# Attention output in a two-layer trunk: V as the stationary operand, weights divided by their sum before the transposes

## The chip, the cores and the metric

The kernel runs on one core of a Trainium2 chip. The metric is device time in microseconds (us). The engines are TensorE (PE, with its weight loads PEld), VectorE (DVE), ScalarE (ACT), GpSimd (POOL) and SyncE (SP, whose queue issues the DMAs here).

## What is computed

A sequence of 512 rows of width 1024 goes through two layers. The first mixes rows with a state-space model, the second with attention of 16 heads of width 64, in three dilated branches whose keys and values are shared. Each layer ends with an MLP. The part that matters is this:

```python
def dilated_branch(q, k_band, v_band, span, dil):
    ...
    s = jnp.einsum('brnqhe,brnkhe->brnhqk', qb, k_band.astype(f32)) * (HEAD_DIM ** -0.5)
    s = jnp.where(band_mask(nb, span)[None, None, :, None], s, NEG)
    m = jnp.max(s, axis=-1, keepdims=True)
    p = jnp.exp(s - m)
    den = jnp.sum(p, axis=-1)
    o = jnp.einsum('brnhqk,brnkhe->brnqhe', p, v_band.astype(f32))
    o = o / jnp.swapaxes(den, 3, 4)[..., None]
    lse = jnp.swapaxes(m[..., 0] + jnp.log(den), 3, 4)
    return from_dilated_blocks(o, seq), from_dilated_blocks(lse, seq)

def dilated_mixer(u, w_q, k_bands, v_bands, w_o):
    ...
    weights = jax.nn.softmax(jnp.stack(lses, axis=-1), axis=-1)
    o = jnp.einsum('gbshe,bshg->bshe', jnp.stack(outs), weights)
    return o.reshape(bsz, seq, BRANCH_WIDTH).astype(u.dtype) @ w_o
```

The softmax over the three branches' log-sums is the same as one softmax over the keys of all three, and the kernel computes it so: one maximum, one exponential and one sum per query row and head.

## The kernel before

Attention is a loop over eight pairs of heads and, in each, over four blocks of 128 queries (`qb` 0 to 3). These 32 steps are called n0 to n31 below. A step has this order on PE, and PE is kept to the order of the code:

- `attn_turn` transposes the exponentials of the step (L1140 for branches 1 and 2, L1142 for branch 0) and has ACT and DVE copy them from PSUM;
- `fill` puts in a share of the projections that the next pairs need (L827 to L829 and L1252 to L1254), as filler;
- `attn_scores` of the following step makes scores for both heads (L1107 for branch 0, L1115 for the others, on tiles of 64 rows by 32 columns). DVE adds the mask and takes the maximum (L1122, L1124), ACT makes exponentials with their sum (L1126), DVE takes the reciprocal of the sums (L1129);
- a second `fill`;
- `turn_back` of the step before: a transpose of its normalised output (L1390), and after the fourth block the copy of the pair's output out of PSUM (L1393);
- `attn_out` multiplies the transposed exponentials with V. For each head there are one (`qb` 0) or two matmuls with 128x128 exponentials as the stationary operand and 64 columns of V moving (L1161, L1163), then eight with 32-column slices of the exponentials stationary, on the four column groups of the array, and 64 columns of V moving (L1167). DVE multiplies the result with the reciprocals (L1169) into the tile `vnat`;
- `late_step` starts one job of the conditioning (adaLN) for the MLP that follows: four DMAs into the tiles `h`, a first product on DVE (L1491), seven more (L1496), a DVE transpose and a sum (L1499, L1500). Jobs run in the first steps of the loop, and a job's loads go into tiles that earlier jobs free.

In the last pair the turn of `fill` differs (a third share stands behind `attn_out`). The order on DVE, ACT and SP is set by a scheduler, not by the code. `self.mark` names the last DVE instruction of `attn_scores`; the subtractions that split weights into two parts (L801) are put behind it. A float32 matmul leaves two records in the trace, a transpose of a full 128 rows or a rounded float32 (`fp32r`) matmul one.

Of the kernel before, what the change touches and what calls it, by code (L numbers as in the profile page):

```python
# [12 lines left out]
ALU = mybir.AluOpType  # L13

P = 128
D = 1024
KT = D // P
T = 512
# [76 lines left out]
class Trunk:  # L95
# [999 lines left out]
    def attn_scores(self, qb, kq):  # L1095


        nc = self.nc
        n = 32 * (qb + 1)
        W = M_W[qb]  # L1100
        heads = [slice(e * 64, e * 64 + 64) for e in range(2)]
        pss = [self.aux_ps() for _ in heads]

        k1, q1 = kq[0]
        for i in range(2 if qb else 1):
            for rows, ps in zip(heads, pss):
                nc.tensor.matmul(ps[:, 2 * n + i * P:2 * n + (i + 1) * P], q1[rows, qb * P:(qb + 1) * P],  # L1107
                                 k1[rows, (qb - i) * P:(qb - i + 1) * P], start=True, stop=True)
        for b in (1, 2):
            kb, q_b = kq[b]  # L1110
            kv_ = kb.rearrange("p (r j) -> p r j", r=4)
            qv = q_b.rearrange("p (r j) -> p r j", r=4)
            for r in range(4):
                for e, (rows, ps) in enumerate(zip(heads, pss)):
                    nc.tensor.matmul(ps[r * 32:(r + 1) * 32, (b - 1) * n:b * n], qv[rows, r, qb * 32:(qb + 1) * 32],  # L1115
                                     kv_[rows, r, 0:n], start=True, stop=True, tile_position=(e * 64, r * 32))

        o = sum(M_W[:qb])
        st = self.t([P, 4, 2], "st", 4)
        out = []  # L1120
        for e, ps in enumerate(pss):
            nc.vector.tensor_tensor_reduce(ps[:, 0:W], ps[:, 0:W], self.msk[:, o:o + W], 1.0, -3e38,  # L1122
                                           ALU.add, ALU.max, st[:, 0, e:e + 1])
            nc.vector.tensor_scalar(st[:, 1, e:e + 1], st[:, 0, e:e + 1], -0.125, None, ALU.mult)  # L1124
            p = self.t([P, T], "sg", 2)
            self.act_mark = nc.scalar.activation(p[:, 0:W], ps[:, 0:W], AF.Exp, bias=st[:, 1, e:e + 1], scale=0.125,  # L1126
                                                 accum_out=st[:, 2, e:e + 1]).ins
            out.append(p)
        self.mark = nc.vector.reciprocal(st[:, 3], st[:, 2]).ins  # L1129
        return out, st  # L1130

    def attn_turn(self, qb, ps, pts):

# [16 lines left out]
            out.append(pt)  # L1150
        return out

    def attn_out(self, pair, qb, pts, st, v, po, on):

        nc = self.nc
        n = 32 * (qb + 1)
        for e, pt in enumerate(pts):
            hd = (2 * pair + e) % 4
            vc = slice(hd * 64, hd * 64 + 64)
            oc = po[:, (2 * qb + e) * 64:(2 * qb + e + 1) * 64]  # L1160
            nc.tensor.matmul(oc, pt[:, 2], v[0][:, qb, vc], start=True, stop=False)  # L1161
            if qb:
                nc.tensor.matmul(oc, pt[:, 3], v[0][:, qb - 1, vc], start=False, stop=False)  # L1163
            for b in (1, 2):
                for r in range(4):
                    rows = slice(r * 32, r * 32 + 32)
                    nc.tensor.matmul(oc[rows], pt[0:n, b - 1, rows], v[b][0:n, r, vc],  # L1167
                                     start=False, stop=(b == 2), tile_position=(0, r * 32))
        nc.vector.tensor_tensor(on.rearrange("p (e c) -> p e c", e=2),  # L1169
                                po[:, qb * P:(qb + 1) * P].rearrange("p (e c) -> p e c", e=2),  # L1170
                                st[:, 3].unsqueeze(2).broadcast_to([P, 2, 64]), ALU.mult)

    def attention(self, adaq, adakv, gate):
        nc, a = self.nc, self.a
# [8 lines left out]
        ow = [None] * KT  # L1183
        kqs, vs, oparts = [None] * KT, [None] * 4, []
# [163 lines left out]
        def fill(t):  # L1348
            state[0] += t
            while state[0] > 0:  # L1350
                c = next(steps, None)
                if c is None:
                    state[0] = 0.0
                    return
                state[0] -= c

        KQ, V = 6 * 8 * 0.64, 16 * 0.64 + 16 * 0.1 + 64 * 0.327
        with self.pinned(nc.tensor):
            fill(0.327 * 15.5)
            self.pumped()  # L1360
            self.table(AF.Exp, self.act_mark)
            fill(KQ + V + AHEAD - 0.327 * 15.5)
            nxt = self.attn_scores(0, kqs[0][0])
            self.heads = True
            turn_back = None
            for pair in range(KT):

                per = (KQ + V * (pair % 2) - LEFT * (pair == KT - 2) if pair < KT - 1 else
                       4 * 7 * 0.64 + LEFT - AHEAD - REST) / 12
                po = self.mm_ps()  # L1370
                parts = PARTS if pair < KT - 1 else PARTS_END
                for qb in range(4):
                    ps, st = nxt
                    pts = self.attn_turn(qb, ps, kqs[pair][1])
                    fill(per * parts[0])
                    if qb < 3:
                        nxt = self.attn_scores(qb + 1, kqs[pair][0])
                    elif pair < KT - 1:
                        nxt = self.attn_scores(0, kqs[pair + 1][0])
                    fill(per * parts[1])  # L1380
                    if turn_back:
                        turn_back()
                        turn_back = None
                    on = self.t([P, P], f"vnat{qb % 2}")
                    self.attn_out(pair, qb, pts, st, vs[pair // 2], po, on)
                    fill(per * parts[2])
                    self.late_step()

                    def turn_back(qb=qb, on=on, po=po, pair=pair):
                        nc.tensor.transpose(po[:, qb * P:(qb + 1) * P], on, self.ident)  # L1390
                        if qb == 3:
                            o = ow[pair] = self.t([P, T], f"h{pair}")
                            nc.vector.tensor_copy(o.rearrange("p (b i r) -> p b r i", b=4, r=4),  # L1393
                                                  po.rearrange("p (b r i) -> p b r i", b=4, r=4))
            fill(1000)
            turn_back()
        self.heads = False
        self.table(AF.Sqrt, self.act_mark)
        split_o(KT - 1)
# [3 lines left out]
        for m in range(4):  # L1403
            w, ps = oparts[m]
# [4 lines left out]
        ps = [self.mm_ps(), self.mm_ps()]  # L1409
# [369 lines left out]
```

## Time and profile before

| | |
|---|---|
| median of 3 runs | 1588.29 us (1586.86 to 1590.06) |
| profiled execution, its own time | 1589.55 us |
| its span in the trace | 1587.7 us |
| PE busy | 1485.6 us, 94% of the span |
| DVE busy | 933.1 us, 59% |
| ACT busy | 569.7 us, 36% |
| the attention loop | about 697 to 1195 us of the span |

The profiled execution is 1.85 us longer than its span, which begins with the first and ends with the last recorded instruction. The busy share of PE is modelled at the ends of matmuls, so starts of rows are the better measure of pace.

### The profile page before, as it was taken

What the parts mean: (1) busy time and instruction counts of PE and PEld (TensorE: products, weight loads), DVE (VectorE), ACT (ScalarE), POOL (GpSimd) and SP (SyncE); (2) the same over time, 40 slices, a digit from 0 to 9 for tenths busy, and PEclk for the clock granted to TensorE, in tenths of its full rate; (3) what the DMA queues carried; (4) which work ended last, traced back from release to release, by engine and by line L of the source; (5) the groups of instructions that cost most, each with busy time, mean ns of one, the idle gap of its engine ahead of it and who ended that gap; (6) DMA issues with size and microseconds to landing.
All of it is one profiled execution on the core that took longest, in us unless ns stands there. A gap on an engine that the chain in (4) does not pass through costs nothing.

```text
span 1587.7 us, 25003 instructions
## 1 busy us (share of the span) xinstructions
PE 1485.6 (94%) x10548; PEld 1248.2 (79%) x10548; DVE 933.1 (59%) x1609; ACT 569.7 (36%) x989; POOL 134.4 (8%) x112
## 2 busy tenths in 40 slices
PE   2567999999999999999899999999998999999998
PEld 1446789888888888977887888888877988888887
DVE  8989995989873445766764323423447634444322
ACT  5657633424242334413322322322344423233222
POOL 8866100000000001000000000000000000000000
PEclk9888999999999999999999999999999999999999
DMA  9313671976643342455552113121324232323301
GB/s 226 130 55 81 180 224 48 317 237 195 204 134 105 106 126 76 123 156 151 160 160 81 54 54 107 54 80 54 101 81 141 90 106 96 106 84 102 106 1 53
DMA packets 214480, 188.45 MB, mean 119 GB/s; under 512 B 7481, under 2 KB 208353, under 8 KB 214369
## 3 DMA queue, kind: packets, MB, share of 16 engines
q1 hardware_dynamic: 214368, 186.87, 38.6%
q8 instruction: 82, 1.34, 0.4%
q14 instruction: 30, 0.24, 0.0%
HBM read 182.66 MB, written 4.19 MB: 118 GB/s over the span
## 4 chain that ended last, share of the span: by engine, by line
PE 78%; DVE 12%; DMA 5%; issue 2%; ACT 1%; SPq 0%; POOL 0%; DVEq 0%; ACTq 0%
PE mm L827 22%; PE mm L829 21%; PE mm L828 21%; DMA W<-in_attn_w_q_dram 2%; DMA h<-in_ada_w_dram 2%; PE mm L1252 1%; PE mm L1253 1%; PE mm L1254 1%; DVE aacc L1496 1%; PE mm L1167 1%; DVE W L801 1%; PE aux L1107 1%; ACT W L799 1%; PE aux L1140 1%; PE mm L1161 1%
## 5 line engine op out<-in xcount | busy, mean ns | idle before, releaser
L799 ACT CAST W<-W 128x1024 fp32r<-128x1024 f32 (+1 forms) x228 | 223.5, 1030 | 397.1 <-PE mm L828 196.5
L827 PE MATMUL mm<-uz,W 128*128 128x512 f32 (+1 forms) x952 | 361.1, 382 | 2.3 <-ACT uz L1308 1.2
L829 PE MATMUL mm<-uz,W 128*128 128x512 f32 (+1 forms) x952 | 359.1, 378 | 3.2 <-DVE W L801 3.2
L801 DVE TENSOR_TENSOR W<-W,W 128x1024 fp32r<-128x1024 f32 (+1 forms) x228 | 266.3, 1197 | 162.7 <-ACT W L799 135.9
L828 PE MATMUL mm<-uz,W 128*128 128x512 f32 (+1 forms) x952 | 358.7, 377 | 2.2 <-DVE uz L749 1.9
L827 PE MATMUL mm<-hid,W 128*128 128x512 f32 (+1 forms) x792 | 299.5, 379 | 0.3 <-ACT hid L1000 0.3
L828 PE MATMUL mm<-hid,W 128*128 128x512 f32 (+1 forms) x792 | 297.0, 375 | 2.5 <-DVE hid L1001 2.5
L829 PE MATMUL mm<-hid,W 128*128 128x512 f32 (+1 forms) x792 | 296.3, 374 | 0.0
L827 PEld LDWEIGHTS mm<-uz,W 128*128 128x128 f32 x952 | 180.1, 189 | 36.9 <-ACT uz L1308 1.6
L829 PEld LDWEIGHTS mm<-uz,W 128*128 128x128 f32 x952 | 180.2, 189 | 36.2 <-DVE W L801 3.6
L828 PEld LDWEIGHTS mm<-uz,W 128*128 128x128 f32 x952 | 180.3, 189 | 34.7 <-DVE uz L749 2.4
L828 PEld LDWEIGHTS mm<-hid,W 128*128 128x128 f32 x792 | 149.7, 189 | 29.2 <-DVE hid L1001 3.1
L827 PEld LDWEIGHTS mm<-hid,W 128*128 128x128 f32 x792 | 149.5, 189 | 27.9 <-ACT hid L1000 0.5
L829 PEld LDWEIGHTS mm<-hid,W 128*128 128x128 f32 x792 | 149.6, 189 | 26.8
L852 DVE SCALAR_TENSOR_TENSOR h<-mm,ada,h 128x512 f32<-128x512 f32 (+1 forms) x77 | 54.2, 708 | 150.6 <-PE mm L829 150.4
L1496 DVE SCALAR_TENSOR_TENSOR aacc<-W,cs,aacc 128x256 f32<-128x256 f32 x196 | 95.6, 488 | 4.0
L1126 ACT ACTIVATE sg<-aux,st 128x192 f32<-128x192 f32 (+3 forms) x64 | 36.6, 577 | 147.2 <-DVE st L1124 141.4
L1252 PE MATMUL mm<-W,hid 128*128 128x256 f32 x256 | 74.6, 292 | 8.4 <-ACT W L1256 8.4
L1029 DVE TENSOR_TENSOR sg<-sg 128x512 f32<-128x512 f32 x64 | 43.8, 688 | 56.9 <-ACT uz L1028 56.7
L1027 ACT ACTIVATE sg<-mm 128x512 f32<-128x512 f32 x60 | 35.6, 595 | 115.8 <-PE mm L829 114.3
L1253 PE MATMUL mm<-W,hid 128*128 128x256 f32 x256 | 73.4, 287 | 0.0
L1254 PE MATMUL mm<-W,hid 128*128 128x256 f32 x256 | 73.4, 287 | 0.0
(333 smaller groups left out, 1746.3 us busy)
## 6 DMA issues: line engine op xcount, KB each, us to landing
W<-in_mlp_w_dram SPq DMA_DIRECT2D x64, 1024.0 KB, 5.3
W<-in_ada_w_dram SPq DMA_DIRECT2D x20, 1024.0 KB, 7.1
h<-in_ada_w_dram SPq DMA_DIRECT2D x64, 256.0 KB, 3.4
W<-in_w_kv_dram SPq DMA_DIRECT2D x12, 1024.0 KB, 5.4
W<-in_w_kv_dram SPq DMA_DIRECT2D x24, 512.0 KB, 4.7
W<-in_attn_w_q_dram SPq DMA_DIRECT2D x24, 512.0 KB, 5.8
W<-in_ssm_w_glu_dram SPq DMA_DIRECT2D x16, 512.0 KB, 5.4
W<-in_kv_ada_w_dram SPq DMA_DIRECT2D x8, 1024.0 KB, 5.6
```

The lines of the kernel that those rows point to most:

```text
L799: h = (nc.gpsimd.tensor_copy if first else nc.scalar.copy)(wh[:, ks], raw[:, ks])
L801: j = eng.tensor_tensor(wl[:, ks], raw[:, ks], wh[:, ks].bitcast(F32), ALU.subtract)
L827: nc.tensor.matmul(o, wh[:, k], uh, start=(start and k == order[0]), stop=False)
L828: nc.tensor.matmul(o, wh[:, k], ul, start=False, stop=False)
L829: self.pe_mark = nc.tensor.matmul(o, wl[:, k], uh, start=False, stop=(stop and k == order[-1])).ins
L852: self.mark = nc.vector.scalar_tensor_tensor(self.h[k][:, cs], src[:, cs], gate[:, k:k + 1], self.h[k][:, cs], ALU.mult, ALU.add).ins
L1029: nc.vector.tensor_tensor(rl, rl, rl, ALU.mult)
L1126: self.act_mark = nc.scalar.activation(p[:, 0:W], ps[:, 0:W], AF.Exp, bias=st[:, 1, e:e + 1], scale=0.125, accum_out=st[:, 2, e:e + 1]).ins
L1252: nc.tensor.matmul(ps[:, j], us[0], wh, start=(k == 0), stop=False)
L1253: nc.tensor.matmul(ps[:, j], us[0], wl, start=False, stop=False)
L1254: nc.tensor.matmul(ps[:, j], us[1], wh, start=False, stop=(k == KT - 1))
L1496: nc.vector.scalar_tensor_tensor(acc, raw[k], self.cs[:, k:k + 1], acc, ALU.mult, ALU.add)
```

## The change

The reciprocal is followed by two DVE multiplications, in place, which divide the exponentials of each head by their sum ahead of the transposes. In `attn_out`, V becomes the stationary operand and the transposed weights move: for branch 0 one or two matmuls per head with 128x64 of V stationary and 128 columns moving, the two heads on the two column halves of the array; for branches 1 and 2, 32 matmuls in place of 16, each with 32 columns of V stationary and 32 columns moving, on the four column groups. The output comes out transposed, so the multiplication behind it (L1169), the tile `vnat` and the transpose of `turn_back` (L1390) go, and the pair's copy out of PSUM stands right behind `attn_out` of the fourth block.

```diff
@@ attn_scores
-        self.mark = nc.vector.reciprocal(st[:, 3], st[:, 2]).ins
-        return out, st
+        nc.vector.reciprocal(st[:, 3], st[:, 2])
+        for e, p in enumerate(out):
+            self.mark = nc.vector.tensor_scalar(p[:, 0:W], p[:, 0:W], st[:, 3, e:e + 1], None, ALU.mult).ins
+        return out
@@ attn_out
-        for e, pt in enumerate(pts):
-            hd = (2 * pair + e) % 4
-            vc = slice(hd * 64, hd * 64 + 64)
-            oc = po[:, (2 * qb + e) * 64:(2 * qb + e + 1) * 64]
-            nc.tensor.matmul(oc, pt[:, 2], v[0][:, qb, vc], start=True, stop=False)
-            if qb:
-                nc.tensor.matmul(oc, pt[:, 3], v[0][:, qb - 1, vc], start=False, stop=False)
-            for b in (1, 2):
-                for r in range(4):
-                    rows = slice(r * 32, r * 32 + 32)
-                    nc.tensor.matmul(oc[rows], pt[0:n, b - 1, rows], v[b][0:n, r, vc],
-                                     start=False, stop=(b == 2), tile_position=(0, r * 32))
-        nc.vector.tensor_tensor(on.rearrange("p (e c) -> p e c", e=2),
-                                po[:, qb * P:(qb + 1) * P].rearrange("p (e c) -> p e c", e=2),
-                                st[:, 3].unsqueeze(2).broadcast_to([P, 2, 64]), ALU.mult)
+        cols = [((2 * pair + e) % 4) * 64 for e in range(2)]
+        for i in range(2 if qb else 1):
+            for e, (pt, c) in enumerate(zip(pts, cols)):
+                nc.tensor.matmul(po[e * 64:e * 64 + 64, qb * P:(qb + 1) * P], v[0][:, qb - i, c:c + 64], pt[:, 2 + i],
+                                 start=(i == 0), stop=False, tile_position=(0, e * 64))
+        for b in (1, 2):
+            for r in range(4):
+                rows = slice(r * 32, r * 32 + 32)
+                for o in range(4):
+                    c = cols[o // 2] + o % 2 * 32
+                    nc.tensor.matmul(po[o * 32:o * 32 + 32, qb * P + r * 32:qb * P + r * 32 + 32],
+                                     v[b][0:n, r, c:c + 32], pts[o // 2][0:n, b - 1, rows],
+                                     start=False, stop=(b == 2 and r == 3), tile_position=(0, o * 32))
@@ the loop
-                    if turn_back:
-                        turn_back()
-                        turn_back = None
-                    on = self.t([P, P], f"vnat{qb % 2}")
-                    self.attn_out(pair, qb, pts, st, vs[pair // 2], po, on)
+                    self.attn_out(pair, qb, pts, vs[pair // 2], po)
+                    if qb == 3:
+                        o = ow[pair] = self.t([P, T], f"h{pair}")
+                        nc.vector.tensor_copy(o.rearrange("p (b i r) -> p b r i", b=4, r=4),
+                                              po.rearrange("p (b r i) -> p b r i", b=4, r=4))
                     fill(per * parts[2])
                     self.late_step()
...
             fill(1000)
-            turn_back()
```

In the changed file the multiplications are L1131, the matmuls of `attn_out` L1163 and L1170, the transposes L1142 and L1144, the job's first product L1482 and the following ones L1487.

On PE, the second `attn_out` of the loop (step n1, `qb` 1) reads as follows before; `mm` is the pair's output in PSUM, and `W` are the tiles of V and of the transposed exponentials.

```order
L1390 MATMUL mm_5732<-cst_63,vnat_684_5825 128x128
L1161 MATMUL mm_5732<-W_5003,W_5459 128x64
L1163 MATMUL mm_5732<-W_5003,W_5459 128x64
L1167 MATMUL mm_5732<-W_5003,W_5459 32x64 x4
L1167 MATMUL mm_5732<-W_5357,W_5459 32x64 x4
L1161 MATMUL mm_5732<-W_5003,W_5459 128x64
L1163 MATMUL mm_5732<-W_5003,W_5459 128x64
L1167 MATMUL mm_5732<-W_5003,W_5459 32x64 x4
L1167 MATMUL mm_5732<-W_5357,W_5459 32x64 x4
L1140 MATMUL aux_5987<-cst_63,sg_5920 96x128 x2
```

The same place after the change, followed as before by the transposes of step n2.

```order
L1163 MATMUL mm_5734<-W_5459,W_5003 64x128 x4
L1170 MATMUL mm_5734<-W_5459,W_5003 32x32 x16
L1170 MATMUL mm_5734<-W_5459,W_5357 32x32 x16
L1142 MATMUL aux_6020<-cst_63,sg_5938 96x128 x2
L1144 MATMUL aux_6020<-cst_63,sg_5938 128x128 x2
```

The transpose of the previous output is gone, the matmuls of branch 0 stand together, and the small ones are 32 in one run.

On DVE, the rows behind the maximum of step n0 are these before; `st` holds the maxima, sums and reciprocals, `aacc` is the sum of an adaLN job, `sg` are the exponentials.

```order
L1124 TENSOR_SCALAR st_5722<-st_5722 128x1 x2
L1491 TENSOR_SCALAR aacc_6703<-h_763_6501,cs_78 128x256
L1496 SCALAR_TENSOR_TENSOR aacc_6703<-h_763_6501,cs_78,aacc_6703 128x256
L1129 RECIPROCAL st_5722<-st_5722 128x2
L1496 SCALAR_TENSOR_TENSOR aacc_6703<-h_764_6503,cs_78,aacc_6703 128x256 x2
L801 TENSOR_TENSOR W_5752<-W_5749,W_5751 128x1024
L1291 COPY W_5643<-mm_5680 128x512
```

After the change, at the same place:

```order
L1124 TENSOR_SCALAR st_5722<-st_5722 128x1 x2
L1482 TENSOR_SCALAR aacc_6796<-h_758_6579,cs_78 128x256
L1487 SCALAR_TENSOR_TENSOR aacc_6796<-h_758_6579,cs_78,aacc_6796 128x256
L1129 RECIPROCAL st_5722<-st_5722 128x2
L1487 SCALAR_TENSOR_TENSOR aacc_6796<-h_759_6581,cs_78,aacc_6796 128x256
L1131 TENSOR_SCALAR sg_5725<-sg_5725,st_5722 128x192
L1131 TENSOR_SCALAR sg_5729<-sg_5729,st_5722 128x192
L1487 SCALAR_TENSOR_TENSOR aacc_6796<-h_759_6581,cs_78,aacc_6796 128x256
```

The two multiplications have come in behind the reciprocal, and the reciprocal stands behind the first product of a job in both. Two steps on, the rows ahead of the maximum of step n2 are these after the change (before it, the job's first product stands behind the reciprocal of n2):

```order
L1482 TENSOR_SCALAR aacc_7201<-h_800_7009,cs_78 128x256
L801 TENSOR_TENSOR W_5904<-W_5901,W_5903 128x1024 x2
L1487 SCALAR_TENSOR_TENSOR aacc_7201<-h_800_7009,cs_78,aacc_7201 128x256
L1294 COPY W_5643<-mm_5819 128x512
L1122 ISA aux_5913,st_5935<-aux_5913,bz_4956 128x448
L1122 ISA st_5935 128x1
```

The first product of a later job now stands ahead of the maximum (L1122) of the step.

## Rows read from the trace of the kernel before

**Rows 1.** Busy time, 840 to 1188: length, PE, PEld, DVE, ACT, POOL, granted clock, DMA.

```profile
840.00:1188.00 348.00, 343.68 (x3384) 288.18 (x3383) 131.66 (x311) 112.68 (x226) 0.00 (x0) 1.00 0.26 76
```

**Rows 2.** PE's waits from 690 to 1200: total, times, longest.

```profile
PE mm L1252 <- ACT W L1256: 8.4, 3, 5.5
PE aux L1140 <- ACT sg L1126: 5.0, 3, 2.6
...
PE aux L1115 <- DVE W L1293: 1.6, 1, 1.6
```

**Rows 3.** Timeline of PE at one attn_out with qb 2: start, duration, records.

```profile
1136.81 0.27 PE L1390 MATMUL mm<-cst,vnat 128*128 128x128 f32 x1
1136.92 0.33 PE L1161 MATMUL mm<-W,W 128*128 128x64 f32 x2
...
1137.41 0.43 PE L1167 MATMUL mm<-W,W 64*32 64x64 f32 x16
1137.77 0.43 PE L1161 MATMUL mm<-W,W 128*128 128x64 f32 x2
...
1138.71 0.42 PE L1140 MATMUL aux<-cst,sg 128*96 128x128 f32 x2
```

**Rows 4.** Timeline of PE at one attn_out with qb 0.

```profile
1053.83 0.27 PE L1390 MATMUL mm<-cst,vnat 128*128 128x128 f32 x1
...
1055.27 0.41 PE L1140 MATMUL aux<-cst,sg 128*64 128x128 f32 x2
```

**Rows 5.** Timeline of PE at two scores, with 32 columns moving and with 64.

```profile
972.89 0.42 PE L1115 MATMUL aux<-W 64*32 64x32 f32 x32
973.24 0.50 PE L827 MATMUL mm<-hid,W 128*128 128x512 f32 x1
...
1042.11 0.45 PE L1115 MATMUL aux<-W 64*32 64x64 f32 x32
1042.49 0.38 PE L1252 MATMUL mm<-W,hid 128*128 128x256 f32 x1
```

**Rows 6.** DVE's groups by shape, 690 to 1200: busy us, mean ns.

```profile
L1169 DVE TENSOR_TENSOR vnat<-mm,st 128x128 f32<-128x128 f32 x32 | 9.3, 289 | 31.1 <-PE mm L1167 31.0
...
L1124 DVE TENSOR_SCALAR st<-st 128x1 f32<-128x1 f32 x64 | 9.1, 150 | 0.6
...
L1491 DVE TENSOR_SCALAR aacc<-h,cs 128x256 f32<-128x256 f32 x13 | 4.6, 352 | 29.0 <-DMA h<-in_ada_w_dram 29.0
```

**Rows 7.** Timeline behind step n0's scores: PE, then DVE; in brackets the wait.

```profile
701.25 0.39 PE L1140 MATMUL aux<-cst,sg 128*32 128x128 f32 x2 [2.64 <-ACT sg L1126]
...
706.87 0.35 DVE L1491 TENSOR_SCALAR aacc<-h,cs 128x256 f32<-128x256 f32 x1 [6.12 <-DMA h<-in_ada_w_dram]
...
707.66 0.16 DVE L1129 RECIPROCAL st<-st 128x2 f32<-128x2 f32 x1
```

**Rows 8.** The chain of waits around the loop's fifth step.

```profile
765.20 7.06 DMA W<-in_attn_w_q_dram
...
774.88 0.58 PE mm L1252
```

**Rows 9.** Timeline at step n17: DVE's reciprocal, PE's first transposes.

```profile
994.55 0.17 DVE L1129 RECIPROCAL st<-st 128x2 f32<-128x2 f32 x1 [1.22 <-ACT sg L1126]
...
995.70 0.41 PE L1140 MATMUL aux<-cst,sg 128*64 128x128 f32 x2
```

**Rows 10.** Timeline at step n27: PE's first transposes, DVE's reciprocal.

```profile
1148.89 0.44 PE L1140 MATMUL aux<-cst,sg 128*128 128x128 f32 x2
...
1149.23 0.16 DVE L1129 RECIPROCAL st<-st 128x2 f32<-128x2 f32 x1
```

**Rows 11.** Timeline behind the last attn_out.

```profile
1190.62 2.36 DVE L801 TENSOR_TENSOR W<-W,W 128x1024 fp32r<-128x1024 f32 x2 [3.53 <-PE mm L1163]
...
1193.75 1.05 DVE L1393 COPY h<-mm 128x512 f32<-128x512 f32 x1 [0.57 <-PE mm L1390]
...
1194.86 0.79 PE L827 MATMUL mm<-uz,W 128*128 128x512 f32 x1 [1.15 <-DVE h L1393]
```

More of the change, by code (lines that the diff above doesn't have):

```diff
@@ L1151, in attn_turn, with attn_out @@
         return out
-    def attn_out(self, pair, qb, pts, st, v, po, on):
+    def attn_out(self, pair, qb, pts, v, po):
         nc = self.nc
         n = 32 * (qb + 1)
-        for e, pt in enumerate(pts):
-            hd = (2 * pair + e) % 4
-            vc = slice(hd * 64, hd * 64 + 64)
-            oc = po[:, (2 * qb + e) * 64:(2 * qb + e + 1) * 64]
-            nc.tensor.matmul(oc, pt[:, 2], v[0][:, qb, vc], start=True, stop=False)
-            if qb:
-                nc.tensor.matmul(oc, pt[:, 3], v[0][:, qb - 1, vc], start=False, stop=False)
-            for b in (1, 2):
-                for r in range(4):
-                    rows = slice(r * 32, r * 32 + 32)
-                    nc.tensor.matmul(oc[rows], pt[0:n, b - 1, rows], v[b][0:n, r, vc],
-                                     start=False, stop=(b == 2), tile_position=(0, r * 32))
-        nc.vector.tensor_tensor(on.rearrange("p (e c) -> p e c", e=2),
-                                po[:, qb * P:(qb + 1) * P].rearrange("p (e c) -> p e c", e=2),
-                                st[:, 3].unsqueeze(2).broadcast_to([P, 2, 64]), ALU.mult)
+        cols = [((2 * pair + e) % 4) * 64 for e in range(2)]
[11 more added lines that the diff above has]
+                                     start=False, stop=(b == 2 and r == 3), tile_position=(0, o * 32))
     def attention(self, adaq, adakv, gate):
@@ L1372, in attention @@
                 for qb in range(4):
-                    ps, st = nxt
-                    pts = self.attn_turn(qb, ps, kqs[pair][1])
+                    pts = self.attn_turn(qb, nxt, kqs[pair][1])
                     fill(per * parts[0])
@@ L1380, in attention @@
                     fill(per * parts[1])
-                    if turn_back:
-                        turn_back()
-                        turn_back = None
-                    on = self.t([P, P], f"vnat{qb % 2}")
-                    self.attn_out(pair, qb, pts, st, vs[pair // 2], po, on)
+                    self.attn_out(pair, qb, pts, vs[pair // 2], po)
[3 more added lines that the diff above has]
+                                              po.rearrange("p (b r i) -> p b r i", b=4, r=4))
                     fill(per * parts[2])
                     self.late_step()
[L1389 to L1394, printed above, removed]
             fill(1000)
-            turn_back()
         self.heads = False
```

## The prediction

> **What bounds the kernel now.** The table gives PE 94% of the span, but that is a mean over stages, so I read the stage of the change first. From 840 to 1188, 23 of the 32 steps, PE is busy 343.68 of 348 us at full clock, DVE 131.66 [rows 1]: there a microsecond less on PE is a microsecond less in all, and DVE counts only where PE waits for it. Next I read what PE waited for in the whole attention loop [rows 2]. The waits lie at the loop's beginning: 8.4 us for a projection's weights (5.5 at once), 5.0 for exponentials (2.6 at once), 1.6 for a copy on DVE ahead of scores. So the loop has two regimes: its first eight steps, where the adaLN jobs, their DMAs and DVE set the pace, and the rest, where PE does. The chain of waits shows what holds the first part: at 765.20 starts a weight DMA of 7.06 us, behind it two steps on ACT, and PE starts its L1252 only at 774.88 [rows 8]. What PE gains or loses before 774.88 vanishes in that wait as long as it is less than the wait.
>
> **What PE saves in a step.** I take starts of rows. With `qb` 2 the block from L1390 to the next step's L1140 goes from 1136.81 to 1138.71, 1.90 us: 0.11 for the transpose of the previous output, 0.49 for four dense records (1136.92 to 1137.41), 0.36 for 16 small ones (1137.41 to 1137.77), and the two once more for the second head [rows 3]. The other blocks with `qb` 1 and 3 have the same records. With `qb` 0 it is 1053.83 to 1055.27, 1.44 us [rows 4].
>
> After the change the block has eight dense records (four with `qb` 0) in two column halves, and 64 small ones (32 matmuls, two records each) with 32 columns moving.
> Dense: four records one after another took 0.49 with one change of tile shape in it, so I take 0.11 for a record and 0.06 for the change. If the two halves run side by side, as column groups do in [rows 3], it is 4 x 0.11 = 0.44 with `qb` 1 to 3 and 0.22 with `qb` 0; one after another, twice that.
> Small: the trace has 32 columns moving in the scores of `qb` 0, where 32 records take 0.35, from 972.89 to 973.24, with the change of shape behind them [rows 5]. That is 0.011 each. 64 records by that price: 0.70, or 0.6 without the second change of shape. This row is the nearest in the columns moving; it has eight tiles in flight where the new code has four. The other end is L1167: four tiles as in the new code, but 64 columns moving, 0.36 for 16 [rows 3]; 64 records by that price are 1.44, and 1.1 without three of the four changes of shape at some 0.1.
> With 0.2 for going into and between the shapes, the new block is 0.44 + 0.6 + 0.2 = 1.24 to 1.28 with `qb` 1 to 3, a saving of 0.62, and 0.22 + 0.6 + 0.2 = 1.02 with `qb` 0, a saving of 0.4. By the other end it is 1.74 and 1.52: a saving of 0.16, and a loss of 0.08.
>
> A rule speaks for the other end. The Trainium skill (TensorEngine Tiling (Array Packing), Instruction Overhead) says that a matmul with one moving column takes as long as one with 60, and that one should not take a tiling factor from a dimension that is small already; the change halves the moving columns from 64 to 32. By that rule 64 records cost four times the 16 of L1167 and the sum is that of the first rival. The trace agrees in part: with eight tiles 32 records with 32 columns moving take 0.35 and with 64 columns 0.38 (1042.11 to 1042.49) [rows 5], almost no gain from fewer columns.
>
> Yet those two rows also say what the limit is. 0.35 for 32 is 0.011 a record, while four tiles with 64 columns go at 0.36 / 16 = 0.0225: if it were a price of each tile, eight tiles would not halve it, and the limit that eight tiles meet is one on issue, which four tiles at 32 columns meet too. I take the lower price.
>
> **Which steps count.** In n0 to n3 the saving falls into the wait at 774.88 [rows 8], in n4 to n7 largely into the wait of 1.6 us for L1293, which the last adaLN job sets [rows 2]. From n8 to n31 nothing else is waited for: 18 steps x 0.62 + 6 x 0.4 = 13.5 us.
>
> **What DVE gets.** Added are 64 multiplications on 192, 384, 448 or 512 columns. The same operation takes 0.150 us on one column and 0.352 on 256 [rows 6], so 0.30, 0.45, 0.50 and 0.55 in a straight line (0.70 for 512 if in proportion): 29 us in all, against 9.3 us of L1169 removed. On an engine that is busy 132 of 348 us this is free except where PE stands right behind it: the transposes now need the reciprocal and a multiplication, and come 0.4 to 0.6 us sooner. At n17 the reciprocal ends at 994.72 and the transposes start at 995.70, 0.98 later [rows 9]; with the transposes 0.4 sooner and a multiplication of 0.45 that just fits. At n27 the transposes start at 1148.89 while the reciprocal ends at 1149.39 [rows 10]. Without L1169 ahead it may end 0.2 sooner, then 0.5 for the multiplication: 1149.7 against 1148.3, a wait of 1.4 us. These two are the tightest that I found from n5 on. I take 1.5 us for all.
>
> **The first steps.** This is where the price may be high. At n0 the transposes start at 701.25, after 2.64 us of wait for the exponentials; the reciprocal they did not need came at 707.66, because on DVE it stands behind L1491, which waits 6.12 us for a job's DMA [rows 7]. In the order of the change the multiplications stand behind that reciprocal and the same wait. So PE's transposes of n0 start at about 707.8 + 0.3 + 0.3, some 708.4: 7.1 us later, and everything on PE behind them, the scores of n1 first. At n2 a job's first product stands ahead of the maximum, so a further 2 to 4 us are likely. Against these 9 to 11 us stand the waits of before, which the lateness takes over: 2.4 of the transposes' 5.0 (those behind the first) and the 5.5 at 774.88 [rows 2], and the savings of n0 to n7 (2 x 0.4 + 6 x 0.62 = 4.5), and at n8 the wait of 1.6. 10 - 2.4 - 5.5 - 4.5 is below zero, so it could all be absorbed; as DVE also has more to do there I leave 2 us, with 0 to 8 as bounds.
>
> **The end.** Behind the last `attn_out`, PE waits for L1169, the transpose and the copy. L801 runs first, from 1190.62, for 2.36 us; the copy starts at 1193.75 and PE's L827 at 1194.86 [rows 11]. In the order of the change L801 still stands ahead of the copy, so the copy starts when L801 ends, at about 1192.9 in these times: 0.85 us sooner, besides the step's own saving.
>
> **Sum.** 13.5 - 1.5 - 2.0 + 0.9 = 10.9 us less. Against the profiled execution's 1589.55 us (its span of 1587.7 and 1.85 around it) that is 1578.6; that execution lies 1.3 above the median of 1588.29, so against the median the gain is 9.7. A measurement of this kernel can tell about 0.2%, 3.2 us, from no change.
>
> **Rivals.**
> 1. The small matmuls keep the pace of L1167. Then n8 to n31 save 18 x 0.16 - 6 x 0.08 = 2.4, with shorter waits (0.9 rather than 1.5) and the same first steps and end: 2.4 - 0.9 - 2 + 0.9 = 0.4 us less, 1589.1: no change. For it speaks that 32 and 64 columns cost almost the same in [rows 5]; against it the halving of the price per record from four to eight tiles.
> 2. The lateness of n0 to n4 is not absorbed, because the projection's weights at 774.88, whose DMA stands in SP's queue among the jobs' loads, come late by the multiplications' delay too. Then up to 8 us stay in place of 2: 4.9 less, 1584.7. Still faster, but within reach of no change.
> 3. With V stationary the column groups do not run side by side. The 64 small records at 0.0225 to 0.03 each become 1.4 to 1.9, and the dense ones 0.88: blocks of 2.5 to 3.0 us instead of 1.9, 0.6 more or worse in each of 24 steps, 14 us and more: about 1604. It decides from 0.02 us for each small record on: (1.9 - 0.44 - 0.2) / 64, at which the block with `qb` 1 to 3 saves nothing even with the halves side by side. Against it: L1167 and L1115 run side by side on the same column groups.
> 4. All of the delay at the beginning and of the new waits is hidden, and blocks fall to 1.15: 16 to 17 us less, 1573.
>
> **Chances.** Forecast 0.50, rival 1 0.17, rival 2 0.16, rival 3 0.09, rival 4 0.08. Faster by over 0.2%: the forecast, rival 4, most of rival 2 (0.12) and a fourth of rival 1 (0.04), 0.74. Slower: rival 3 and a little of rivals 1 and 2, 0.11. The rest, 0.15, is no change. The range goes from 1572, past rival 4, to 1590, which takes in rivals 1 and 2 and leaves out rival 3 and a fringe; the forecast's own is 1575 to 1583.
>
> **What would show it.** Right: in the steady part the block from the first L1163 to the next transposes is about 1.2 to 1.3 us, with L1170's 64 records in 0.55 to 0.7; PE's transposes of n0 start at about 708.4; the L1252 that started at 774.88 is within 3 us of it; one wait of 1 to 2 us for a multiplication at n27; the copy L1383 follows L801 at the end. Wrong: L1170 over 1.0 us a block (rival 1), waits of PE for DVE's multiplications in many steps, or L1252 coming at 780 or later (rival 2).

## The result and the profile after

The changed kernel takes 1572.03 us (median of 4 runs, 1571.05 to 1573.65) against 1589.03 us of the kernel before in the same comparison: 17.0 us less, a ratio of 0.9892 with a 95% interval of 0.988 to 0.9904. I had forecast faster, by 10 us, at 1578.6; the time lies at the very edge of the range of 1572 to 1590, and the ratio, taken to the 1588.29 of the kernel before, gives 1571.1, just under it. The profiled execution is 1572.7 us with a span of 1570.9, so 16.8 us of span have gone.

First the waits, as in [rows 2]: what PE waited for in the attention loop after the change, with the total, the number and the longest.

```profile
PE aux L1142 <- DVE sg L1131: 13.9, 5, 9.3
PE mm L827 <- DVE h L1383: 2.7, 1, 2.7
PE aux L1115 <- DVE W L1294: 2.6, 1, 2.6
...
PE mm L1163 <- ACT W L1257: 0.3, 1, 0.3
```

Two things are to be seen. The transposes now wait 13.9 us for the multiplications, 9.3 at once. And the 8.4 us of L1252 for the ACT copy L1256 are gone: that line is L1253 now, and it is not in the list. That was in no part of my forecast.

The block of `qb` 2, on PE, as in [rows 3]: start, duration, records.

```profile
1064.56 0.39 PE L828 MATMUL mm<-hid,W 128*128 128x512 f32 x1
1064.79 0.39 PE L829 MATMUL mm<-hid,W 128*128 128x512 f32 x1
1065.10 0.66 PE L1163 MATMUL mm<-W,W 128*64 128x128 f32 x8
1065.69 0.76 PE L1170 MATMUL mm<-W,W 64*32 64x32 f32 x64
1066.38 0.42 PE L1142 MATMUL aux<-cst,sg 128*96 128x128 f32 x2
```

The 64 small records take 0.69 us, 0.011 each, and the eight dense ones 0.59, so the two column halves run side by side. The block starts 0.31 after the filler's last matmul, where the filler's own step is 0.23; with these 0.08 it is 1.36 us against 1.90. Of the 0.54 saved, the transpose of the turn is 0.11 and the dense records with their changes of shape 0.40 (0.67 for 1.07 in [rows 3]); the small records give 0.03 (0.69 for 0.72). With `qb` 0, on PE:

```profile
1043.82 0.28 PE L1255 MATMUL mm<-W,hid 128*128 128x256 f32 x1
1044.03 0.44 PE L1163 MATMUL mm<-W,W 128*64 128x128 f32 x4
1044.40 0.75 PE L1170 MATMUL mm<-W,W 32*32 32x32 f32 x64
1045.09 0.41 PE L1142 MATMUL aux<-cst,sg 128*64 128x128 f32 x2
```

1.06 us from the first L1163, and 0.09 of a later start, 1.15 against 1.44 [rows 4].

Behind the first scores, DVE and PE in order of time, as in [rows 7]:

```profile
706.13 0.35 DVE L1482 TENSOR_SCALAR aacc<-h,cs 128x256 f32<-128x256 f32 x1 [5.51 <-DMA h<-in_ada_w_dram]
...
706.92 0.16 DVE L1129 RECIPROCAL st<-st 128x2 f32<-128x2 f32 x1
...
707.44 0.54 DVE L1131 TENSOR_SCALAR sg<-sg,st 128x192 f32<-128x192 f32 x2
707.81 0.61 PE L1142 MATMUL aux<-cst,sg 128*32 128x128 f32 x2 [9.27 <-DVE sg L1131]
```

PE stands 9.27 us because the multiplications stand behind a job's first product, which waits for its DMA. The multiplications themselves are cheap: DVE's groups by shape, 690 to 1190.

```profile
L1131 DVE TENSOR_SCALAR sg<-sg,st 128x512 f32<-128x512 f32 x16 | 7.1, 483 | 0.2
...
L1131 DVE TENSOR_SCALAR sg<-sg,st 128x192 f32<-128x192 f32 x16 | 4.4, 318 | 0.2
```

24.0 us in all, for 9.3 of L1169 [rows 6].

**Where the 16.8 us come from, by place.** I compare the starts of scores (L1107). Those of n9 start at 854.54 before and at 853.56 after, 1.0 sooner. Those of n31, in the timeline of the kernel before:

```profile
1179.19 0.72 PE L1107 MATMUL aux<-W 64*128 64x128 f32 x8
```

And in that of the changed kernel:

```profile
1166.13 0.72 PE L1107 MATMUL aux<-W 64*128 64x128 f32 x8
```

13.1 sooner, so 12.1 us come from n9 to n31. The last 3.8 come behind that. In the 12.1 there are 22 blocks (6 x 0.29 + 16 x 0.54 = 10.4), less the one wait for a multiplication at n27, 1.55, which leaves 8.8; of the other 3.3 us, 2.9 are two waits of L1252 of 1.1 and 1.8 us at n13 and n21, part of the 8.4, which have gone. This is the first of them in the kernel before, PE, ACT and DVE in order of time:

```profile
911.03 1.99 ACT L799 CAST W<-W 128x1024 fp32r<-128x1024 f32 x2
...
911.42 1.04 PE L1239 MATMUL mm<-cst,rstd 128*128 128x128 f32 x8
...
912.91 0.59 ACT L1256 COPY W<-mm 128x512 f32<-128x512 f32 x1
...
913.56 0.39 PE L1252 MATMUL mm<-W,hid 128*128 128x256 f32 x1 [1.10 <-ACT W L1256]
...
919.37 1.08 DVE L1393 COPY h<-mm 128x512 f32<-128x512 f32 x1 [4.90 <-PE mm L1390]
```

And the same place after the change:

```profile
896.15 1.09 DVE L1383 COPY h<-mm 128x512 f32<-128x512 f32 x1
...
908.19 2.00 ACT L799 CAST W<-W 128x1024 fp32r<-128x1024 f32 x2
...
908.60 1.03 PE L1240 MATMUL mm<-cst,rstd 128*128 128x128 f32 x8
...
909.39 0.36 PE L1253 MATMUL mm<-W,hid 128*128 128x256 f32 x1
...
910.07 0.60 ACT L1257 COPY W<-mm 128x512 f32<-128x512 f32 x1
```

ACT does the same in the same order: a cast of 2 us, then the copy of a finished product out of PSUM. Before, PE's next product waits for that copy; after, it starts 0.68 ahead of it. Every projection takes one of four PSUM buffers (`mm_ps` has `bufs=4`), and so does a pair's output `po`. Before, `po` of the finished pair is copied out at 919.37, behind the turn in the next pair's first `attn_out`; after, at 896.15, right behind its own. So a buffer is free one step sooner. That is theory A below; the rival, B, is that the shorter blocks merely shifted ACT's copies.

### The profile page after: what moved, and what is told of

The parts are those of the page before. It is cut to its first block, busy times and chain, and to the rows that moved or that the text cites. A ratio compares the mean times of both kernels' runs of the same rounds, so it can differ in the third digit from the quotient of the medians.

```text
span 1570.9 us, 27064 instructions
## 1 busy us (share of the span) xinstructions
PE 1468.5 (93%) x11540; PEld 1228.3 (78%) x11540; DVE 945.9 (60%) x1641; ACT 569.4 (36%) x989; POOL 134.1 (9%) x112
## 4 chain that ended last, share of the span: by engine, by line
PE 73%; DVE 15%; DMA 7%; issue 3%; ACT 1%; SPq 1%; POOL 0%; DVEq 0%; ACTq 0%
PE mm L827 21%; PE mm L829 20%; PE mm L828 20%; DMA h<-in_ada_w_dram 3%; DVE aacc L1487 2%; DVE W L801 2%; DMA W<-in_attn_w_q_dram 2%; PE mm L1253 1%; PE mm L1254 1%; PE mm L1255 1%; DMA W<-in_mlp_w_dram 1%; PE mm L1170 1%; ACT W L799 1%; PE aux L1142 1%; PE aux L1107 1%
## 5 line engine op out<-in xcount | busy, mean ns | idle before, releaser
L801 DVE TENSOR_TENSOR W<-W,W 128x1024 fp32r<-128x1024 f32 (+1 forms) x228 | 265.6, 1196 | 159.1 <-ACT W L799 137.2
L1487 DVE SCALAR_TENSOR_TENSOR aacc<-W,cs,aacc 128x256 f32<-128x256 f32 x196 | 95.5, 487 | 4.0
L1253 PE MATMUL mm<-W,hid 128*128 128x256 f32 x256 | 73.4, 287 | 0.0
L1254 PE MATMUL mm<-W,hid 128*128 128x256 f32 x256 | 72.4, 283 | 0.0
L1255 PE MATMUL mm<-W,hid 128*128 128x256 f32 x256 | 72.4, 283 | 0.0
```

What stands on the lines that cost most here:

```text
L801: j = eng.tensor_tensor(wl[:, ks], raw[:, ks], wh[:, ks].bitcast(F32), ALU.subtract)
L1253: nc.tensor.matmul(ps[:, j], us[0], wh, start=(k == 0), stop=False)
L1254: nc.tensor.matmul(ps[:, j], us[0], wl, start=False, stop=False)
L1255: nc.tensor.matmul(ps[:, j], us[1], wh, start=False, stop=(k == KT - 1))
L1487: nc.vector.scalar_tensor_tensor(acc, raw[k], self.cs[:, k:k + 1], acc, ALU.mult, ALU.add)
```

## The experiments

**The change in three steps.** The first, e4, puts the multiplications into the kernel before and nothing else.

```diff
-        self.mark = nc.vector.reciprocal(st[:, 3], st[:, 2]).ins
+        nc.vector.reciprocal(st[:, 3], st[:, 2])
+        for e, p in enumerate(out):
+            self.mark = nc.vector.tensor_scalar(p[:, 0:W], p[:, 0:W], st[:, 3, e:e + 1], None, ALU.mult).ins
...
-        nc.vector.tensor_tensor(on.rearrange("p (e c) -> p e c", e=2),
...
+        nc.vector.tensor_copy(on, po[:, qb * P:(qb + 1) * P])
```

> The kernel before with the two multiplications ahead of the transposes and a plain copy in place of the multiplication L1169; products and transposes back as before. It carries the DVE side of the change alone. Theory A (they cost one wait of about 1.5 us late in the loop and 7 us at n0, of which the jobs' pace hides most): 1589 to 1593, with L1252's waits changed by at most the lateness. Theory B (they cost nothing, or the changed order on DVE even helps): 1585 to 1588.

Measured: 1594.19 against 1587.71 us, a ratio of 1.0037 (1.0023 to 1.0051): 6.5 us slower, above what either theory said. PE's waits in it:

```profile
PE aux L1142 <- DVE sg L1131: 15.4, 4, 11.8
PE mm L1252 <- ACT W L1256: 7.0, 3, 4.1
```

The wait at n0 is 11.8 us, yet the wait of L1252 fell only from 5.5 to 4.1. The lateness of the first steps is 7 us at n1 to n5 and 5.0 from n6 on; another 1.5 come at n27 and n28. ACT shows why so little was absorbed:

```profile
777.66 0.57 ACT L1126 ACTIVATE sg<-aux,st 128x384 f32<-128x384 f32 x1
...
778.21 1.99 ACT L799 CAST W<-W 128x1024 fp32r<-128x1024 f32 x2
780.09 0.59 ACT L1256 COPY W<-mm 128x512 f32<-128x512 f32 x1
```

L1256 stands behind the cast, the cast behind the exponentials of n5, and these wait for DVE, which waits for a job's DMA. The copy that PE waits for came late along with everything else, so 5.0 of the 7 us stay, as the second rival has it, though not by way of its weight DMA.

The second step, e7, is the changed kernel with the pair's buffer held as long as before.

```diff
+                            if pair < KT - 1:
+                                self.after(i.ins, self.out_mark, mybir.DependencyClass.Sync)
```

Here `i` is the copy of a finished pair and `out_mark` a matmul of the next step's `attn_out`.

> The changed kernel, but the copy of a pair's output out of PSUM (pairs 0 to 6) depends on the next step's attn_out, so that it runs where the kernel before had it and the pair's bank stays taken one step longer. Theory A (the bank): PE waits for the ACT copy L1257 ahead of its next projection in the second steps of pairs 1, 3 and 5 as before, 1 to 2 us each at n13 and n21, up to 5 at n5; time 3 to 6 us above the changed kernel's, 1574 to 1578. Theory B (the waits went for another reason): no such wait and a time within 1.5 us of the changed kernel's.

Measured: 1581.34 against 1587.71, 0.9954 (0.9936 to 0.9972). PE's waits:

```profile
PE aux L1142 <- DVE sg L1131: 13.9, 5, 9.0
PE mm L1254 <- ACT W L1258: 8.2, 3, 5.4
```

The three waits are back: 8.2 us in three, where it was 8.4 in three [rows 2], and the time is 9.3 us above the changed kernel's, more than I expected. This shows theory A: in the code nothing differs but what the copy waits for and the place where it is written, which by itself does nothing (e1 below), and the waits for the multiplications are 13.9 us as in the changed kernel. The 9.3 us are not simply the three waits. At the scores of n9 only 2.9 us of the first are left, as e7 comes to n5 2.0 us sooner and loses 1.9 less at n8; n13 costs 1.3. The wait of 1.8 us at n21 costs 3.5, because a stretch at half clock (1.2 of 2.4 GHz) follows it, which the kernel before does not have behind its own wait of 1.8. This is the window behind it in e7, the granted clock third from the end:

```profile
1044.00:1049.00 5.00, 5.00 (x30) 5.00 (x31) 0.82 (x1) 2.82 (x4) 0.00 (x0) 0.66 0.49 130
```

And the window behind the same wait in the kernel before:

```profile
1048.00:1053.00 5.00, 5.00 (x44) 5.00 (x44) 0.52 (x1) 2.53 (x4) 0.00 (x0) 1.00 0.44 114
```

The scores of n31 start at 1173.82, 7.7 later than in the changed kernel; the rest of the 9 us is lost behind the loop, in waits at the next norm.

So the ladder of spans is 1587.7, with the multiplications 1594.0 (+6.3), with the products turned round and the turn back gone 1579.7 (-14.3), with the early copy 1570.9 (-8.8). These are single profiled executions; by the ratios of medians the three steps are some +5.9, -13.2 and -9.8 us.

**The buffer alone, and a try that did nothing.** e2 takes the kernel before and turns a pair's fourth block back at once.

```diff
+                    if qb == 3 and pair < KT - 1:
+                        turn_back()
+                        turn_back = None
```

> The kernel before, but the transpose and copy of a pair's fourth block stand right behind its attn_out in pairs 0 to 6; nothing else of the change. Theory A (bank): L1252's waits fall from 8.4 to under 1.5 us; PE pays a wait for L1169 of 0.5 to 0.8 us seven times, so the time moves little, between 1585 and 1590. Theory B: L1252 still waits about 8 us and the time rises by the waits for L1169, 3 to 5 us, to 1592 to 1594.

Measured: 1585.38 against 1589.49, 0.9977 (0.9967 to 0.9986). L1252 waits for L1256 no more; PE pays for it with waits for L1169, 8.7 us in eight, of which 4.0 at the end of the first pair, and 2.3 at the end of the loop that were there before:

```profile
PE mm L1390 <- DVE vnat L1169: 8.7, 8, 4.0
```

Theory A again. In e1 I moved only the place in the code at which the copy is written, one step later, as before the change.

```diff
+                    if copy_out:
+                        copy_out()
+                        copy_out = None
                     self.attn_out(pair, qb, pts, vs[pair // 2], po)
```

> The changed kernel, but the copy of a pair's output out of PSUM stands one step later, where the kernel before had it (the last pair's stays where the change put it). Theory A (the pair's PSUM bank is free one step sooner, and that is what took away the waits of L1252 on the ACT copy L1256, 8.4 us in three before): the waits of L1253 on L1257 come back at the second step of pairs 1, 3 and 5, 3 us of them in the steady part and up to 5 at the first; time 3 to 8 us above the changed kernel's, 1575 to 1580. Theory B (the waits went because the blocks are shorter and the order on ACT fits better): no such wait, time within 1.5 us of the changed kernel.

Measured: 1571.86 us, as the changed kernel (0.9892, 0.9876 to 0.9907), with no wait for L1257 over 0.7. This doesn't speak for B: the scheduler put the copy on DVE where its input is ready, as early as without the edit (896.15), so the edit did not do what it was meant to. It is e7's dependency that holds the copy back.

```profile
895.05 1.08 DVE L1391 COPY h<-mm 128x512 f32<-128x512 f32 x1
```

**What the multiplications cost inside the change.**

```diff
-        for e, p in enumerate(out):
-            self.mark = nc.vector.tensor_scalar(p[:, 0:W], p[:, 0:W], st[:, 3, e:e + 1], None, ALU.mult).ins
```

> The changed kernel without the two multiplications: the division by the sum is left out. Theory A (the multiplications cost PE one wait of 1.55 us at n27, and what they cost before n8 is hidden behind the adaLN jobs): the wait behind n0's scores falls from 9.3 to about 2.6 us, the scores of n8 still end at 835 to 836, and the time falls by 1.5 to 3 us to 1569 to 1570.5. Theory B (the multiplications also cost in the first steps): n8 comes 3 us sooner or more, and the time falls by 5 to 8 us.

Measured: 1576.1 us, 0.9917 (0.99 to 0.9934): 4 us more than with the multiplications, which neither theory allowed. The scores of n31 start 0.8 sooner than in the changed kernel, and n0's wait is 3.4. But n8 gives it back:

```profile
PE aux L1140 <- ACT sg L1126: 10.0, 5, 3.4
PE aux L1115 <- DVE W L1292: 7.2, 1, 7.2
```

PE came to n8 early and waited 7.2 us there behind the last job, in place of 2.6. So 5.7 us of span are lost behind n31: the half clock behind the pair's copy lasts some 3 us longer, at the next norm PE waits 1.3 and 1.5 us against 0.4 in the changed kernel, and then it has the half clock again for 3.4 us (0.66 granted from 1215 to 1220). So the multiplications are hidden in the changed kernel as long as the jobs hold n8; that what is lost behind the loop comes from DVE's order there is argued, not shown.

**The small matmuls.** e5 puts them on the column halves, with half as many records.

```diff
-                for o in range(4):
-                    c = cols[o // 2] + o % 2 * 32
...
+                for e, c in enumerate(cols):
+                    nc.tensor.matmul(po[e * 64:e * 64 + 64, qb * P + r * 32:qb * P + r * 32 + 32],
+                                     v[b][0:n, r, c:c + 64], pts[e][0:n, b - 1, rows],
+                                     start=False, stop=(b == 2 and r == 3), tile_position=(0, e * 64))
```

> The changed kernel with the matmuls of branches 1 and 2 on the two column halves: 16 with 64 columns of V stationary and 32 moving in place of 32 with 32 stationary; 32 records a block in place of 64. If a record has a price of its own on issue (0.011 us, as L1170's 64 in 0.69 us): 0.35 us a block, the block 0.35 us shorter and one change of shape less, time 1561 to 1565. If the limit is one of each tile (weight load or moving columns): 16 records on each half at 0.04 to 0.055 us, 0.65 to 0.9 us a block, time 1570 to 1577.

Measured: 1578.27 us, 0.9937 (0.9919 to 0.9954). The block with `qb` 2 on PE:

```profile
1064.66 0.66 PE L1163 MATMUL mm<-W,W 128*64 128x128 f32 x8
1065.25 1.12 PE L1169 MATMUL mm<-W,W 64*64 64x32 f32 x32
1066.31 0.42 PE L1142 MATMUL aux<-cst,sg 128*96 128x128 f32 x2
```

Half the records take 1.06 us in place of 0.69, and the time is above both forecasts. The limit is one of each tile, not one of each record: 16 records on a tile take 0.69 with 32 columns of V stationary and 1.06 with 64, at the same 32 columns moving. The starts of single records in the traces say which columns count. On one tile they lie 32 to 33 ns apart in the changed kernel (32 columns stationary, 32 moving), 58 in e5 (64 and 32) and 56 in L1167 of the kernel before (32 and 64). So the price grows with the stationary columns and with the moving ones alike; whether the two add up or the larger one decides, these runs do not separate. What I took for a limit on issue is this, and that its price came out right is luck.

**The jobs' order.** The first eight steps go at the pace of the adaLN jobs, before and after. e6 orders each job's first product behind the multiplications of the step that starts it; e8 does the same to the kernel before.

```diff
-            if not self.jobs_started:
+            if late or not self.jobs_started:
                 self.jobs_started = True
                 self.after(i.ins, self.mark)
```

> The changed kernel, but each adaLN job's first product is ordered on DVE behind the multiplications of the step in which it is started, so one job a step and no multiplication or maximum behind a job's wait for its DMA of the same step. Theory A (the jobs, bunched in n0 to n8, are what PE waits for there, 9.3 us at n0, 1.2, 1.9 and 2.6 us): most of these waits go, the scores of n8 end 5 to 12 us sooner, time 1560 to 1567. Theory C (the projections' weights, which share the DMA queue, set the pace of the first steps): n8 comes within 2 us of the changed kernel's, time 1570 to 1574.

> The kernel before with the order of the adaLN jobs of e6_job_order: each job's first product behind the reciprocals of its step. Against e6_job_order it shows what the change is worth once the jobs no longer hold the first eight steps. Theory A: 24 blocks by 0.54 and 8 by 0.29 us, 15.3, plus L1252's three waits of up to 8 us in all, plus 1 to 2 us at the end, less some 5 us of waits for multiplications: 18 to 22 us slower than e6_job_order, 1579 to 1583, with L1252 waiting 6 to 9 us. Theory C (the order helps only with the multiplications in the way, the kernel before has nothing to gain from it): 1587 to 1590.

Measured: e6 1560.86 against 1589.49, 0.9823 (0.9808 to 0.9838); e8 1570.95 against 1587.71, 0.9891 (0.9875 to 0.9907). Both are theory A in kind; e8 is 8 us faster than the least I expected. PE's waits in e6:

```profile
PE aux L1142 <- DVE sg L1131: 7.3, 3, 3.3
```

And in e8:

```profile
PE mm L1252 <- ACT W L1256: 2.9, 2, 1.8
PE mm L1390 <- DVE vnat L1169: 2.3, 1, 2.3
```

With the jobs out of the way, the wait of 5.5 us at n5 is gone in the kernel before as well: it needed the held buffer and the jobs together. That the jobs come in by way of ACT is read from e4 and not tested by itself. With that order the change is worth some 10 us (1570.95 to 1560.86). It is worth less than in the old order because the multiplications cost more: from the scores of n9 to those of n31 it gains 6.0 us where it gained 12.1, as the waits for L1131 at n17 and n27, 3.3 and 1.6 us, cost about 4.7 and 3.1 with the half clock behind them. In the changed kernel the two were 0.2 and 1.55. The first in e6:

```profile
973.87 0.61 PE L1142 MATMUL aux<-cst,sg 128*64 128x128 f32 x2 [3.29 <-DVE sg L1131]
```

What made the first grow is open: DVE's L801, which waits for a cast on ACT, stands ahead of the maximum there and starts 4.2 us after the scores, against 1.1 in the changed kernel. And the jobs' order alone takes as much off the kernel before as the change does, 17 us.

e10 separates the buffer in this order: e6 with e7's dependency.

> e6_job_order with the copy of e7_copy_waits: jobs in order, but the pair's PSUM bank held one step longer as before the change. Theory A (in the steady part the early copy is worth the two waits of 1.1 and 1.8 us at n13 and n21, and at n5 it mattered only because the jobs held the weights up): waits of PE on L1258 of 2.5 to 3.5 us in all, time 1563 to 1566. Theory B (the bank costs at n5 too, whatever the jobs do): 5 us more there, time 1567 to 1571.

Measured: 1565.59, 0.985 (0.9834 to 0.9866): 4.7 us above e6, with waits of 4.0 in two and a stretch of half clock behind the first.

```profile
PE mm L1254 <- ACT W L1258: 4.0, 2, 2.2
```

Theory A in its place, with waits a little above its 2.5 to 3.5 us: some 5 of the change's 10 us are the buffer.

**A try for the end of the loop.** e9 is e6 with the MLP's first weight splits L801 behind the last pair's copy.

```diff
+            if self.behind is not None:
+                self.after(j.ins, self.behind)
...
+            if k == KT - 1:
+                self.behind = j.ins
```

> e6_job_order, and the weight splits L801 of the MLP that follows are ordered on DVE behind the last pair's copy and its split, so that the copy no longer stands behind 2.4 us of L801. Theory A: the copy starts 1.5 to 2 us sooner after the last attn_out, PE waits about 1 us for it in place of 2.7, and the stretch at the half clock behind it gets shorter or goes; 2 to 4 us in all, time 1557 to 1559. Theory B (what is put back there comes late for the MLP, or the gain is lost in the waits at the norm that follows): within 1.5 us of e6_job_order.

Measured: 1562.63, 0.9834 (0.9817 to 0.985), no faster than e6. PE's waits from 1160 to 1210 in it:

```profile
PE mm L829 <- DVE h L1387: 1.1, 1, 1.1
PE aux L965 <- DVE rcol L961: 1.1, 1, 1.1
PE aux L958 <- ACT aacc L869: 0.9, 1, 0.9
```

The wait for the copy fell from 2.7 to 1.1 as expected, but PE waits at the norm that follows, and the wait at n17 is 4.3 in place of 3.3. That is theory B, though the time is 1.8 us above e6, a little outside its 1.5. e6 stays the fastest version: 28.6 us under the kernel before.

## Why the prediction was right in sign and too small

**The saving of a block** was 13.5 in the sum; it is 18 x 0.54 + 6 x 0.29 = 11.5. The price of the small records held (0.011), though not for the reason I gave, and the column halves run side by side. With `qb` 2, the dense records and the changes of shape ahead of them and behind take 0.67 for my 0.64, the small ones 0.69 with the change behind them for my 0.6: the change of shape at the end of the block is what I had left out. The first rival is out: 64 records take 0.69 us, where by L1167's 16 in 0.36 [rows 3] they would take 1.44. The Trainium skill's rule (TensorEngine Tiling (Array Packing), Instruction Overhead), that a matmul with one moving column takes as long as one with 60, doesn't agree with this: with 32 stationary columns in both, records on one tile start 56 ns apart in L1167 with 64 moving columns and 32 to 33 in L1170 with 32. L1167's 0.0225 had the changes of shape of a short run in it besides. The third rival is out too.

**The multiplications** in the steady part were -1.5, and the one wait at n27 is 1.55; n17 fits as forecast. DVE's lines took 0.32 us for 192 columns (0.30 forecast) and 0.48 for 512 (0.55).

**The first steps** were -2.0, with 0 to 8 as bounds. Here the reasoning failed, though the transposes of n0 start at 707.81, where I had said 708.4. I let the lateness vanish in the wait at 774.88, reading from [rows 8] that a weight DMA set it. e4 shows that with the multiplications something else sets it: the copy that PE waits for stands behind the exponentials of n5, which come late with the rest, and 5.0 us stay. In the changed kernel this is undone because the wait itself is gone, and n9 comes 1.0 sooner; in e7, with the wait back, n9 comes 1.9 later than in the kernel before, by luck close to the 2.0 of the sum.

**"From n8 to n31 nothing else is waited for"** is the step that failed. [rows 2] gives 8.4 us in three waits with 5.5 the longest, so 2.9 were left, and I never looked up where: they lie at n13 and n21, so two of the three were wrongly put at the loop's beginning. Nor did I ask what a PE matmul waits for when it waits for an ACT copy of another product, a PSUM buffer. With that, the diff's moved copy would have been a term: in the sum it had the end of the loop alone, 0.9. e7 prices it at 9.3 us, from waits of 8.2 in all, of which some are taken up later and one brings a stretch at half clock.

**The end** gave 3.8 us: two blocks (1.1), 1.2 for L1169 and the turn on the way to the copy (0.9 forecast), and 1.5 that I had not counted, from a shorter stretch at half clock and a shorter wait at the norm.

In short, the mechanism that I forecast is there, at 11.5 for 13.5. On top came a second one, a buffer freed a step sooner, which I had read past; and the cost of the multiplications, which I put at 3.5, is 6.5 in the kernel before. Term by term in the changed kernel, with the forecast in brackets: blocks 11.5 (13.5), multiplications -1.55 (-1.5), first steps +1.0 (-2.0), end 2.7 besides its blocks (0.9), waits at n13 and n21 2.9 (nothing); that is 16.6 of the 16.8 us.

## What to carry to other kernels

When a change moves a copy out of PSUM, list the waits of later matmuls for copies of other products: here they were waits for a buffer, and freeing one a step sooner took all three away. A wait can absorb lateness only if what ends it doesn't come late too; follow its chain one engine further than the DMA. And before tuning a step, see whether something unrelated sets the pace around it: here a one-line order for the adaLN jobs was worth as much as the whole change.

## What the runs showed of the hardware

Sixteen matmul records on one column tile took 0.69 us with 32 stationary columns and 1.06 us with 64, with 32 moving columns in both. From start to start they lie 32 to 33 and 58 ns apart, and 56 with 32 stationary and 64 moving columns. After the last `attn_out` PE waits for the copy, and the granted clock is half of full speed (1.2 of 2.4 GHz) for a while. Windows of the kernel before, with the granted clock third from the end of a row:

```profile
1195.00:1200.00 5.00, 5.00 (x12) 3.94 (x13) 2.60 (x3) 2.44 (x3) 0.00 (x0) 0.51 0.25 86
1200.00:1205.00 5.00, 5.00 (x23) 4.11 (x23) 2.67 (x5) 0.64 (x1) 0.00 (x0) 1.00 0.64 204
```

Windows of the changed kernel:

```profile
1180.00:1182.50 2.50, 2.50 (x7) 1.93 (x7) 0.69 (x1) 0.18 (x2) 0.00 (x0) 0.50 0.84 290
1182.50:1185.00 2.50, 2.50 (x11) 2.01 (x11) 1.45 (x2) 1.97 (x2) 0.00 (x0) 0.96 0.16 57
```

Seven matmuls in 2.5 us against eleven. Before, PE had waited 2.3 and 1.15 us and the half clock held to 1200; after, it had waited 2.73 and the half clock held to 1182.5. The same wait need not end the same: behind 1.8 us at n21 the clock was full in the kernel before and at half for 3.4 us in e7 (the two windows above). In e9, where it waited 1.1, the clock stayed full:

```profile
1168.00:1172.00 4.00, 3.96 (x17) 3.29 (x18) 2.96 (x3) 0.62 (x1) 0.00 (x0) 1.00 0.95 302
```
